# One scheduling change to a two-layer decoder step on eight cores: per-queue transfer model, moved norm, bigger weight packets

**Chip, cores, metric.** One Trainium2 chip, eight cores, each working on one prompt sequence of 2048 rows and 64 rows of decode samples; nothing is exchanged between cores. The metric is the device time of the slowest core in microseconds. Most executions agree within 0.3%.

## The reference

```python
def hybrid_layer(x, ...):
    h = rms_norm(x, norm_g)
    p = h @ w_in                                   # 1024 -> 3456 columns
    a_val, a_gate, a_z, b_h, b_b, b_c, b_z, c_u, c_v, c_z = split(p)
    # group A: GLU, causal depthwise conv of width 31, LayerNorm over 384 channels
    y_a = silu(layer_norm(causal_dwconv(a_val * sigmoid(a_gate)) + bias)) * silu(a_z)
    # group B: gated conv of width 3
    y_b = b_b * causal_dwconv3(b_c * b_h) * silu(b_z)
    # group C: LayerNorm of c_v, 128x128 causal position mixing per chunk
    y_c = c_u * chunk_mix(layer_norm(c_v)) * silu(c_z)
    return x + concat(y_a, y_b, y_c) @ w_out, ...   # plus new conv states
# two layers, then a final rms_norm; prompt and samples
```

## The kernel before

Each layer goes through the rows in five blocks of up to 512 rows. A block takes x, norms it (H_elem), transposes it (T, on TensorE), and multiplies h by pieces of w_in (stages A, Bz, AZ, CV, B, C); the GLU output goes through HBM to build the operand of the width-31 convolution; at the end mix is multiplied by w_out (stage_O), one block late. A seam is the passage from one block to the next. In the lines of the profile xr is x, h_tm and h_fm are h before and after the transposes, nv is the normed c_v, a_t the GLU output, a_scr its copy in HBM, A the operand of the width-31 convolution, and as_ext and zst are the histories of convolutions A and B for the samples; the engines are PE (TensorE), ACT (ScalarE), DVE (VectorE), GpSimd (POOL) and SP, which issues DMA. The program is written as a list of statements with reads and writes. A greedy scheduler then orders each engine's instructions by simulated times, and only that order is built.

```python
    def order(self):
        ...
        dma_free = 0.0
        while len(out) < n:
            # per engine: of the next LOOK statements that are ready, the one that can start first
            ...
            if op.dma:
                issue = 100.0 if e != "pool" else 1000.0
                free[e] = st + issue
                dstart = max(st + 1300.0, dma_free)
                dma_free = dstart + op.nbytes / 190.0      # ONE stream for all queues
                fin = dma_free + 900.0
            else:
                free[e] = st + op.cost
                ...
```

```python
        def H_elem(l, blk):                       # the norm of a block
            for j, (t, r, c0) in enumerate(blk.tiles):
                act(h_tm[...], xr[...], AF.Square, ..., accum=ss[...])   # ACT
                rsq(rstd[...], ss[...], ...)                             # GpSimd: add, pow
                ts(h_tm[...], xr[...], rstd[...], ...)                   # DVE

        def hist_dma(l, after=()):                # conv histories of the samples
            ... as_ext <- st_aT (GpSimd queue), scaled on DVE
            dma("sp", zst[:], st_bT[l], [], ["zst"], after)
            cp(zs_ext[...], zst[...], ..., eng="pool")                   # GpSimd cast

        def params_comp(l, after=()):
            S.add("pool" if l else "dve", W4 = idh32 * wc4, cost=7000 if l else 3300)   # 128x3072
```

```python
        for oi, (l, blk) in enumerate(order_b):
            stage_A(l, blk)
            a4 = [a4_load(l, blk, c, False) for c in range(3)]
            if prev is not None: stage_LN(*prev, pcb)
            ...
            stage_Bz; stage_AZ
            if prev is not None: stage_O(*prev)
            ... # loads: x of the next block; w_out in the very first block
            stage_CV(l, blk)
            mC = mark()
            if blk.first: hist_dma(l, mC)
            if nxt is not None: H_elem(*nxt)      # norm of the next block
            for c in range(3): stage_B(l, blk, c)
            stage_C(l, blk)
            if nxt is not None:                   # the seam to the next block
                convs(..., [0]); T(*nxt, 0); T(*nxt, 1)
                convs(..., [1, 2]); T(*nxt, 2); T(*nxt, 3)
                convs_smp(...)
                stage_stats(l, blk)
```

## Time and profile before

| | before |
|---|---|
| median of the first three runs | 671.95 us (671.85 to 711.28) |
| span of the cores in the profile | 662.3 to 672.4 us, median 665.9 |
| TensorE (PE) busy, slowest core | 610.5 us of 672.4 |
| PE idle between its first transposes and its last matmul, median core | about 41 us |
| start of the first w_out stage, median core | 127.4 us |

The page and the waits are read in the prediction below, with their lines. In the page's rows each digit is a fortieth of the span in tenths; a line of PE's timeline is start, length, engine, line, operation, shapes, count, and in brackets the idle time before it with what ended it. I use the start of each w_out stage as a milepost: its matmuls are easy to find in every trace, and PE does the same work between two of them in both kernels.

### The profile page before, as it was taken

What the parts mean: (1) busy time and instruction counts of PE and PEld (TensorE: products, weight loads), DVE (VectorE), ACT (ScalarE), POOL (GpSimd) and SP (SyncE); (2) the same over time, 40 slices, a digit from 0 to 9 for tenths busy, and PEclk for the clock granted to TensorE, in tenths of its full rate; (3) what the DMA queues carried; (4) which work ended last, traced back from release to release, by engine and by line L of the source; (5) the groups of instructions that cost most, each with busy time, mean ns of one, the idle gap of its engine ahead of it and who ended that gap; (6) DMA issues with size and microseconds to landing.
All of it is one profiled execution on the core that took longest, in us unless ns stands there. A gap on an engine that the chain in (4) does not pass through costs nothing.

```text
span 672.4 us, 11366 instructions; the slowest of 8 cores (662.3 to 672.4 us)
## 1 busy us (share of the span) xinstructions
PE 610.5 (91%) x4452; PEld 329.0 (49%) x4452; DVE 395.9 (59%) x742; ACT 251.8 (37%) x432; POOL 94.8 (14%) x163
## 2 busy tenths in 40 slices
PE   1779759999999999999989998999989999999974
PEld 0334324455556555555534543455545655655631
DVE  1273423964485566586485542896269576664764
ACT  3311326402630640651454034622462373272622
POOL 1601030210031011001240400121011002100101
PEclk9998959999999999999999999999979999999977
DMA  8999785842796079089494983521642033313202
GB/s 193 135 223 165 146 120 133 184 132 46 168 195 156 1 160 225 15 234 229 129 171 119 202 146 109 114 95 38 176 117 95 17 118 102 101 44 55 96 0 94
DMA packets 64053, 83.97 MB, mean 125 GB/s; under 512 B 8128, under 2 KB 54912, under 8 KB 64000
## 3 DMA queue, kind: packets, MB, share of 16 engines
q1 hardware_dynamic: 41600, 59.56, 31.2%
q0 software_dynamic: 18176, 19.24, 21.4%
q10 hardware_dynamic: 4224, 4.46, 2.6%
q8 instruction: 35, 0.57, 0.3%
q14 instruction: 18, 0.15, 0.1%
HBM read 80.59 MB, written 27.62 MB: 161 GB/s over the span
## 4 chain that ended last, share of the span: by engine, by line
PE 79%; DMA 8%; ACT 5%; DVE 4%; POOL 2%; issue 2%; SPq 0%; POOLq 0%; ACTq 0%; DVEq 0%; another core or an unknown queue 0%
PE pb L442 70%; PE pb L443 6%; DMA w_in_sb<-w_in 5%; PE pb L560 2%; DMA xr<-x_scr 2%; DMA xr<-x_in 2%; ACT tmp L402 1%; ACT L402 1%; DVE tmp L422 1%; ACT h_tm L402 1%; POOL w_in_sb L432 1%; DVE h_fm L415 1%; ACT cbh L402 1%; ACT vb L402 1%; DVE mix L410 0%
## 5 line engine op out<-in xcount | busy, mean ns | idle before, releaser
L442 PE MATMUL pb<-h_fm,w_in_sb 128*128 128x384 bf16 (+2 forms) x2000 | 374.5, 347 | 18.3 <-ACT tmp L402 4.6
L442 PEld LDWEIGHTS pb<-h_fm,w_in_sb 128*128 128x128 bf16 x2000 | 194.7, 99 | 185.6 <-issue 15.9
L402 ACT ACTIVATE tmp<-pb 128x384 f32<-128x384 f32 (+2 forms) x110 | 57.3, 522 | 264.1 <-PE pb L442 254.7
L442 PE MATMUL pb<-w_out_sb,mix 128*128 128x512 bf16 (+1 forms) x544 | 122.1, 385 | 4.0 <-DVE mix L410 4.0
L442 PEld LDWEIGHTS pb<-w_out_sb,mix 128*128 128x128 bf16 (+1 forms) x544 | 54.1, 100 | 69.8 <-DVE mix L410 4.4
L410 DVE TENSOR_TENSOR xr<-pb,xr 128x512 f32<-128x512 f32 (+1 forms) x68 | 46.5, 688 | 43.2 <-PE pb L442 43.0
L538 POOL TENSOR_SCALAR rstd<-ss 128x1 f32<-128x1 f32 (+1 forms) x47 | 12.6, 269 | 317.9 <-ACT h_tm L402 187.4
L410 DVE TENSOR_TENSOR mix<-tmp 128x384 bf16<-128x384 f32 (+2 forms) x50 | 30.0, 601 | 30.8 <-ACT tmp L402 30.6
L443 PE MATMUL pb<-A,W 128*32 128x384 bf16 (+2 forms) x1152 | 47.9, 314 | 0.1
L402 ACT ACTIVATE h_tm<-xr 128x1024 bf16<-128x1024 f32 (+1 forms) x34 | 35.6, 1049 | 11.0 <-DMA xr<-x_in 6.3
L422 DVE SCALAR_TENSOR_TENSOR tmp<-z_ext,pc,tmp 128x384 f32<-128x384 bf16 (+1 forms) x60 | 38.9, 658 | 1.2
L402 ACT ACTIVATE tmp<-xr 128x1024 bf16<-128x1024 f32 (+1 forms) x17 | 18.0, 1057 | 55.4 <-DVE xr L410 55.4
L422 DVE SCALAR_TENSOR_TENSOR tmp<-pb,pc,mean_b 128x384 f32<-128x384 f32 (+2 forms) x30 | 18.6, 652 | 33.9 <-ACT mean_b L402 33.9
L415 DVE TENSOR_SCALAR h_fm<-pb,pc 128x384 bf16<-128x384 bf16 (+2 forms) x40 | 17.2, 437 | 34.6 <-PE pb L560 32.7
L410 DVE TENSOR_TENSOR tmp<-pb,tmp 128x384 f32<-128x384 f32 (+2 forms) x50 | 29.6, 593 | 10.3 <-PE pb L442 9.6
L443 PEld LDWEIGHTS pb<-A,W 128*32 128x32 bf16 x1152 | 25.6, 96 | 20.0 <-issue 4.0
L422 DVE SCALAR_TENSOR_TENSOR a_t<-tmp,pb 128x384 bf16<-128x384 f32 (+1 forms) x30 | 16.4, 559 | 27.8 <-ACT tmp L402 27.5
L757 DVE RECIPROCAL vb<-vb 128x384 f32<-128x384 f32 (+2 forms) x10 | 27.9, 2793 | 7.7 <-ACT vb L402 7.6
L415 DVE TENSOR_SCALAR h_tm<-xr,rstd 128x1024 bf16<-128x1024 f32 (+1 forms) x34 | 25.1, 748 | 11.8 <-POOL rstd L539 7.8
L442 PE MATMUL pb<-w_in_sb,h_fm 128*128 128x256 bf16 (+1 forms) x272 | 31.6, 273 | 0.0
L402 ACT ACTIVATE h_fm<-pb,pc 128x384 bf16<-128x384 bf16 (+2 forms) x40 | 24.2, 614 | 17.3 <-PE pb L560 14.7
L402 ACT ACT_TABLE_LOAD x22 | 28.2, 1283 | 5.0 <-DMA xr<-x_in 4.7
(73 smaller groups left out, 457.4 us busy)
## 6 DMA issues: line engine op xcount, KB each, us to landing
A<-a_scr SPq DMA_DIRECT2D x96, 103.0 KB, 5.3
w_in_sb<-w_in POOLq DMA_DIRECT2D x17, 512.0 KB, 21.6
xr<-x_in SPq DMA_DIRECT2D x16, 512.0 KB, 10.0
x_scr<-xr SPq DMA_DIRECT2D x16, 512.0 KB, 5.3
xr<-x_scr SPq DMA_DIRECT2D x16, 512.0 KB, 7.9
y_o<-xr SPq DMA_DIRECT2D x16, 512.0 KB, 2.7
w_out_sb<-w_out POOLq DMA_DIRECT2D x4, 1024.0 KB, 18.7
w_in_scr<-w_in POOLq DMA_DIRECT2D x7, 512.0 KB, 13.2
```

The lines of the kernel that those rows point to most:

```text
L402: S.add("act", lambda e: e.activation(out=out, in_=in_, func=func, **kw), reads=reads, writes=writes, cost=170 + 0.833 * free_size(out) + ...
L410: S.add(eng, lambda e: e.tensor_tensor(out=out, in0=a, in1=b, op=op), reads=reads, writes=writes, cost=velem(eng, out, 1))
L415: S.add(eng, lambda e: e.tensor_scalar(out, a, s1, None, op0), reads=reads, writes=writes, cost=velem(eng, out, fast))
L422: S.add(eng, lambda e: e.scalar_tensor_tensor(out=out, in0=a, scalar=s, in1=b, op0=op0, op1=op1), reads=reads, writes=writes, cost=velem(e ...
L432: S.add(q, lambda e: e.dma_start(out=out, in_=in_), reads=reads, writes=writes, dma=True, nbytes=n * (2 if in_.dtype == BF16 else 4), afte ...
L442: return lambda e: e.matmul(out, lhsT, rhs, start=start, stop=stop)
L443: return lambda e: e.matmul(out, lhsT, rhs, start=start, stop=stop, tile_position=tp)
L538: S.add("pool", lambda e: e.tensor_scalar(out, in_, EPS, None, ALU.add), reads=rk, writes=wk, cost=300)
L560: pe([(lambda e, k=k, j=j, r=r, c0=c0: e.transpose(V[:, k % 2, c0:c0 + r], h_tm[0:r, j, k * 128:(k + 1) * 128], ident_bf[0:r, 0:r])) for k ...
L757: S.add("dve", lambda e: e.reciprocal(vb[:, 0:n], vb[:, 0:n]), reads=["vb"], writes=["vb"], cost=90 + 6.4 * n)
```

## The change

Its intent: let the scheduler believe that each queue's transfers run by themselves, move block 1's norm behind the second of three B steps, move histories and w_out of layer 0 later, start the first block with two of its four tiles, load w_in in packets twice as long, hide later seams (third convolution behind the transposes, statistics in the next stage A), and put the first tap of convolution B on ACT. Cut to its core:

```diff
+GW = [2, 4]          # groups per w_in piece, per layer (was 4, 4): 2048 B packets in layer 0
+GO = [8, 8]
+    RATE = {"sp": 180.0, "pool": 250.0, "act": 150.0}
-        dma_free = 0.0
+        dma_free = {}
-                dstart = max(st + 1300.0, dma_free)
-                dma_free = dstart + op.nbytes / 190.0
-                fin = dma_free + 900.0
+                dma_free[e] = max(st + 1300.0, dma_free.get(e, 0.0)) + op.nbytes / self.RATE[e]
+                fin = dma_free[e] + 900.0
...
-            dma("sp", zst[:], st_bT[l], [], ["zst"], after)
+            dma("sp", zst[:], st_bT[l], [], ["zst"], after if l else ())
...
-                ts(o, win(0), colA(l, c, 3), None, ALU.mult, ...)          # tap 0 on DVE
+                act(o, win(0), AF.Copy, ..., scale=colA(l, c, 3))          # on ACT
...
         for t in blocks[0].ids:
-            load_x(0, t)
+            load_x(0, t, (), "act" if t % 2 else "sp")
-        H_elem(0, blocks[0])  ... all four tiles, then the projections
+        H_elem(0, blocks[0], (), (0, 1))   ... two halves, each with half-width projections
...
-            stage_A(l, blk)
+            stage_A(l, blk, (lambda: stage_stats(*prev)) if prev is not None else None, ...)
-            if blk.first:
+            if blk.first and l:
                 hist_dma(l, mC)
-            if nxt is not None:
+            late = l == 0 and blk.first
+            if late:
+                pass
+            elif nxt is not None:
                 H_elem(*nxt)
             for c in range(3):
                 stage_B(l, blk, c)
+                if late and c == 1:
+                    H_elem(*nxt, mark())
+            if blk.first and l == 0:
+                hist_dma(l, mD)            # w_out of layer 0 likewise, behind stage_C
             stage_C(l, blk)
...
-                convs(l, blk, a4, pcb, [1, 2])
+                convs(l, blk, a4, pcb, [1])
                 T(*nxt, 2)
                 T(*nxt, 3)
+                convs(l, blk, a4, pcb, [2])
                 convs_smp(l, blk, a4, pcb, [0, 1, 2])
-                stage_stats(l, blk)
```

## The prediction

> **What bounds the kernel now.** I read the page first, then the spans of the cores, the waits of TensorE (PE), PE's timeline over the first 135 us and around the later seams, and the table of stretches.
>
> ```profile
> span 672.4 us, 11366 instructions; the slowest of 8 cores (662.3 to 672.4 us)
> PE 610.5 (91%) x4452; PEld 329.0 (49%) x4452; DVE 395.9 (59%) x742; ACT 251.8 (37%) x432; POOL 94.8 (14%) x163
> PE   1779759999999999999989998999989999999974
> PEclk9998959999999999999999999999979999999977
> DMA  8999785842796079089494983521642033313202
> ```
>
> PE is the bound, in every slice from the seventh on. The change removes no matmul of weight, so the only thing to win is PE's idle time, 672.4 - 610.5 = 62 us, and the time at the lower clock (digits 5 and 7 in the PEclk row). The first six slices, 0 to 101 us, hold most of both, and there the DMA row is full. The waits of PE say who ends the gaps:
>
> ```profile
> PE pb L560 <- DVE h_tm L415: 9.8, 1, 9.8
> PE pb L873 <- DVE ident_bf L426: 8.6, 1, 8.6
> PE pb L873 <- DVE h_tm L415: 7.5, 3, 5.6
> PE pb L442 <- ACT tmp L402: 4.6, 3, 3.3
> PE pb L442 <- DVE h_fm L415: 4.2, 4, 1.1
> PE pb L442 <- DVE mix L410: 4.0, 1, 4.0
> PE pb L442 <- DMA w_in_sb<-w_in: 4.0, 2, 3.8
> ```
>
> PE's timeline puts them in time (start, length, instructions, idle before):
>
> ```profile
> 22.78 9.22 PE L442 MATMUL pb<-h_fm,w_in_sb 128*128 128x512 bf16 x32 [2.58 <-ACT h_fm L402]
> 50.27 7.03 PE L442 MATMUL pb<-h_fm,w_in_sb 128*128 128x512 bf16 x24 [3.75 <-DMA w_in_sb<-w_in]
> 90.20 4.87 PE L560 MATMUL pb<-ident_bf,h_tm 128*128 128x128 bf16 x32 [9.82 <-DVE h_tm L415]
> 492.42 7.88 PE L442 MATMUL pb<-h_fm,w_in_sb 128*128 128x384 bf16 x30 [3.30 <-ACT tmp L402]
> 649.45 13.36 PE L442 MATMUL pb<-w_out_sb,mix 128*128 128x512 bf16 x48 [4.03 <-DVE mix L410]
> ```
>
> So there are five places: the first projection cannot start before 22.78; it runs dry of w_in at 46.5; the seam from block 0 to block 1 of layer 0 costs 9.82; a dozen seams of about 1 us each; and the tail. In the table of stretches (PE, PEld, DVE, ACT and POOL busy, granted clock, DMA share, GB/s) the seam has a second cost:
>
> ```profile
> 80.00:85.00 5.00, 0.38 (x2) 0.00 (x0) 1.68 (x4) 4.58 (x9) 2.53 (x5) 1.00 0.01 4
> 90.00:95.00 5.00, 4.80 (x32) 2.73 (x32) 1.56 (x4) 2.33 (x4) 0.00 (x0) 0.50 1.14 168
> 95.00:100.00 5.00, 3.97 (x15) 1.78 (x15) 0.90 (x2) 0.21 (x1) 0.00 (x0) 0.62 1.18 167
> ```
>
> PE waits while ACT squares block 1 (4.58 of 5 us) and DMA is idle (0.01): x landed long before, and the squares merely stand behind the last Silu of block 0 in ACT's order. Afterwards the clock is 0.50 and 0.62.
>
> **What the Trainium skill says.** (1) "TensorE: Matmul & The Clock Gate", Part 1: PE falls to half clock after about 3.4 us of idleness and needs about 3.4 us of work to return. The trace agrees: after gaps of 9.82, 3.75, 3.30 and 4.03 us the clock reads 0.50 to 0.68, after the gaps of 0.8 to 1.8 us it stays 1.00. (2) "DMA: Bandwidth & Descriptors", Issuing engines are not separate DMA queues: transfers from several engines share the same 16 DMA engines. The trace agrees: from 20 to 75 us the DMA share is 1.03 to 1.18 whoever issued, so moving x loads to ACT's queue reorders bytes and makes no bandwidth. (3) The same page, Why small descriptors are slow: a fixed cost per packet. The trace has it: cast packets of w_in take a median of 98 ns at 1024 B written and 134 ns at 1536 B, which is about 26 ns fixed plus 36 ns per 512 B written (per 1 KB of f32 read). (4) "ScalarE: Activation LUTs", What ACT_TABLE_LOAD costs: 1283 ns. The trace: 22 of them, 1283 ns mean.
>
> **The change part by part.**
>
> *Startup and w_in.* Now x0 lands at 4.65 but x1 only at 12.75 and x2 at 14.83, and the projection waits for all four tiles. After, x1 goes out at once on ACT's queue, and two tiles are normed, transposed and projected before the other two. From x1's landing (estimate 7 to 9) the chain is table load 1.28, two squares of 1.25, two roots, two scalings of 0.75, a transpose and half-width evictions: about 8.5 us, so the first half projection starts near 16 to 17. That is 6 us earlier, but the second half of its weights is piece 1, which may only be loaded once x2 is there; it landed about 25 us before, and I expect 21 to 22. So PE starts early, then waits; the 32-matmul stretch ends near 30 instead of 32.0. Then w_in: halving its packets (g of 4 becomes 2) makes one of 2 KB written cost about 26 + 144 = 170 ns instead of two of 98. A 512 KB piece is 512 x 98 / 16 = 3.1 us now and 256 x 170 / 16 = 2.7 us after; eleven pieces and the big one drop from 38.8 to 33.8 us. As a check, between 15.1 and 76.8 us all traffic (w_in 38.8, block 1's x 4.5, A loads 10.5, as_ext 4.4, rest of x and parameters 3.5) adds up to 61.7 us: that stretch is one saturated DMA. The as_ext load (4.4) is also moved behind it. Piece 6, which PE lacked at 46.5 until 50.13, then lands at 46 to 49, with the A loads of the first channel newly ahead of it. PE would ask for it near 44.5: a stall of about 3 us remains. Later pieces are no longer short. The 1.21 wait for nv goes because stage B now stands before it. Sum here: 4.5 us (2 to 8).
>
> *The seam to block 1.* H_elem of block 1 now comes after the second of three stage-B steps, so ACT's 4 x 1.24 us, POOL's 4 x 0.8 and DVE's 4 x 0.75 lie beside the third B step (3.5), the mixing (0.6), a convolution (1.9) and two CU/CZ stages (7.2), 13 us of PE. Gone: 9.82 idle, the 1.04 for h_fm, and the slow clock. The last is: from 90.20 to 100.57 PE did 32 transposes and 16 matmuls, which at full clock are 32 x 63 ns + 16 x 194 ns = 5.1 us; it took 10.4, less the 1.04 gap, so 4.2 us. Sum 15.1; I take off 1.5, since as_ext now lands about when DVE wants it, just ahead of the h_fm evictions: 13.5 (9 to 15).
>
> *Other seams.* The third convolution moves behind the last transposes and covers their evictions (1.04, 1.13 and 1.04 us at 168, 405 and 474). The statistics move into the next block's stage A: 0.80 twice and 0.28 four times. That is 5.9; I count 5. The 3.30 at 492 is ACT waiting for a late x1 load inside its order with tanh behind it. The new order has the squares after tanh and Silu, so that goes too, with its slow clock (30 matmuls at 263 ns for 176, 2.6 us), but only core 3 has it, and it is why core 3 is 6 us above the median core.
>
> *First tap of conv B on ACT.* 30 DVE operations of about 0.43 us become ACT operations of about 0.5 us. Neither engine bounds; in the tail DVE is the chain, and three taps less are about 1 us of its 4.03. But one tap there waits in ACT behind the Silu of the LayerNorm. I count 0.7.
>
> *Costs added.* Half-width matmuls add about 32 weight loads, beside the matmuls; new ACT waits in front of tanh 1 us.
>
> **Sum.** The median core is at about 666: 666 - 4.5 - 13.5 - 5 - 0.7 + 1 = 643. The slowest core was 6 above the median; without core 3's special gap I expect 2, so 645, 4% faster.
>
> **Rivals.** *The weights bind anyway.* If w_in arrives no sooner (packets twice as long at the same bytes per second; A loads earlier in the stream), PE starts early and waits longer at pieces 1 and 6, and the startup part is zero, with a slow clock behind a stall over 3.4 us. For it: the share above 1 all the way. Against it: the fixed 26 ns and the removed as_ext. Time: 650. *A wait takes the place of the seam's.* as_ext is issued about 67 us, behind w_in in the same queue, and took 18 us to land before. DVE would then block in front of h_fm, and PE stall 5 us, clock included. For it: that landing time. Against it: its own work is 4.4 us and the queue is nearly empty by then. Time: 651. *ACT becomes the new seam.* The taps and the moved statistics put ACT work in front of tanh and Silu at ten seams; 1 us more at each takes back the small seams. ACT at 40% speaks against. Time: 653. *All goes well*, piece 6 included: 634.
>
> **Range and chances.** Centre 645. The seam alone, the surest part, is 2%; startup and small seams rarely fail together. 8 in 10: 635 to 657. Faster than 2% means below 658.5: 0.93; within 2%: 0.06; slower: 0.01.
>
> **What would show it.** Right: first 256-column matmuls near 16 to 17 us; PE waiting for w_in once or twice by 3 us or less; no gap over 2 us around 75 to 85 us and PEclk 1.00 there; no wait of PE for h_fm or cbh after 110 us; PE busy down to about 600, mostly from the clock; packets of 2048 B in w_in's queue near 170 ns. Wrong: a w_in wait of over 4 us, a gap ended by h_fm with as_ext behind it, waits for ACT tmp above 6 us in sum, or a clock of 0.5 in the first 60 us that was not there before.

## The result

The changed kernel: 648.54 us median of 12 runs (645.23 to 757.17; two slow), against 672.92 us for 15 runs of the kernel before. Executions in which one die ran at a lower clock are left out of the means. The ratio of the fast runs is 0.9642, 95% interval 0.9624 to 0.966. A ratio is always the mean time of one kernel's fast runs over that of the kernel before in the same rounds, so not quite the ratio of the medians; where I turn ratios into microseconds below, I multiply by 673.

The page of the changed kernel, the same rows as those of the kernel before in the prediction:

```profile
span 645.6 us, 11435 instructions; the slowest of 8 cores (640.7 to 645.6 us)
PE 603.4 (93%) x4484; PEld 330.6 (51%) x4484; DVE 379.2 (59%) x710; ACT 269.1 (42%) x472; POOL 92.9 (14%) x163
PE   1799989999899999999989999999999999999973
PEclk9999979999999999999999999999999999999977
DMA  8999888625956395199597862531633062224102
```

The low digits of the PE row up to 100 us (before: 7, 7, 7 and 5 in slices 2, 3, 5 and 6) are gone but for slice 2, which holds the start, and an 8 in slice 6, PE's busy time fell by 7 us (I put it down to the clock, by the first digits of PEclk), and the DMA row still shows 8 and 9 up to about 110 us. PE's waits (total, times, longest) on the same core, 6, without the start's 12.3 and 1.7:

```profile
PE pb L444 <- DMA w_in_sb<-w_in: 4.7, 2, 2.9
PE pb L444 <- DVE mix L412: 4.0, 1, 4.0
PE pb L445 <- DMA A<-a_scr: 3.8, 1, 3.8
PE pb L444 <- ACT tmp L404: 3.5, 2, 1.8
PE pb L444 <- DVE a_t L424: 2.3, 1, 2.3
```

The 9.8 us for the norm of block 1 is gone, and so are the waits for h_fm on DVE. Two are new: 3.8 us for a convolution operand, and two of 1.8 us for a tanh on ACT (the kernel before had three ended by ACT tmp, 4.6 us in sum). PE's timeline puts them in time:

```profile
17.12 3.50 PE L444 MATMUL pb<-h_fm,w_in_sb 128*128 128x256 bf16 x16 [2.90 <-DMA w_in_sb<-w_in]
22.92 1.92 PE L444 MATMUL pb<-h_fm,w_in_sb 128*128 128x256 bf16 x16 [1.85 <-DMA w_in_sb<-w_in]
83.61 3.60 PE L445 MATMUL pb<-A,W 128*32 128x512 bf16 x32 [3.75 <-DMA A<-a_scr]
167.58 7.97 PE L444 MATMUL pb<-h_fm,w_in_sb 128*128 128x384 bf16 x48 [1.77 <-ACT tmp L404]
336.42 1.89 PE L444 MATMUL pb<-h_fm,w_in_sb 128*128 128x512 bf16 x8 [2.27 <-DVE a_t L424]
```

The first projection comes at 17.12 instead of 22.78, but PE then waits twice for weights. The tail's 4.0 (the wait for mix) is what it was. The gap at 80 to 83.6 us is nearly core 6's own: two other cores show 0.3 and 1.1 us there, five none, and the traces of a3, b2, b3 and f1 below, with nearly the same loads, show none on any core, while b1 has one of 3.4 us on core 1: it comes in some executions. It brings back the slow clock, as the table of stretches shows (PE, PEld, DVE, ACT and POOL busy, granted clock, DMA share, GB/s):

```profile
80.00:85.00 5.00, 1.40 (x16) 0.59 (x20) 0.79 (x2) 0.81 (x2) 0.00 (x0) 0.69 1.20 216
85.00:90.00 5.00, 5.00 (x36) 1.83 (x29) 0.00 (x0) 1.37 (x2) 0.00 (x0) 0.63 1.18 177
```

At the same place the kernel before had a DMA share of 0.01, here it is 1.20: the seam is no longer held by an order of instructions, but where it is held, by the transfers.

The mileposts, medians of the eight cores' traces, in us:

| | before | after | won so far |
|---|---|---|---|
| first projection | 23.4 | 17.2 | 6.2 |
| end of block 0's projections | 78.8 | 77.0, with a convolution of 1.85 already done | 3.7 |
| first w_out stage | 127.4 | 108.3 | 19.1 |
| second | 190.9 | 172.1 | 18.8 |
| fourth | 301.0 | 281.7 | 19.3 |
| fifth | 364.4 | 346.2 | 18.2 |
| sixth | 433.2 | 410.9 | 22.3 |
| tenth | 643.6 | 620.3 | 23.3 |
| span | 665.9 | 642.1 | 23.8 |

So four fifths of the gain are there by the first w_out stage, and all later seams together bring about 4 us, nearly all of it between the fifth and sixth stage, where the seam from block 0 to block 1 of layer 1 lies (near 405 us before). What brought those 4 us is shown under b4 below.

### The profile page after: what moved, and what is told of

The parts are those of the page before. It is cut to its first block, busy times and chain, and to the rows that moved or that the text cites. A ratio compares the mean times of both kernels' runs of the same rounds, so it can differ in the third digit from the quotient of the medians.

```text
span 645.3 us, 11435 instructions; the slowest of 8 cores (640.7 to 645.6 us)
## 1 busy us (share of the span) xinstructions
PE 604.7 (94%) x4484; PEld 331.6 (51%) x4484; DVE 381.4 (59%) x710; ACT 269.2 (42%) x472; POOL 95.0 (15%) x163
## 4 chain that ended last, share of the span: by engine, by line
PE 86%; DMA 6%; ACT 3%; DVE 2%; issue 1%; SPq 0%; POOLq 0%; POOL 0%; ACTq 0%; DVEq 0%
PE pb L444 76%; PE pb L445 7%; DMA xr<-x_in 4%; PE pb L568 3%; DMA w_in_sb<-w_in 1%; ACT tmp L404 1%; ACT L404 1%; DMA A<-as_scr 1%; DVE tmp L424 1%; DVE vb L776 0%; ACT vb L404 0%; DVE tmp L412 0%; SPq L434 0%; DVE mix L412 0%; ACT mean_b L404 0%
## 5 line engine op out<-in xcount | busy, mean ns | idle before, releaser
L444 PE MATMUL pb<-h_fm,w_in_sb 128*128 128x384 bf16 (+3 forms) x2032 | 371.6, 342 | 13.1 <-DMA w_in_sb<-w_in 5.6
L444 PEld LDWEIGHTS pb<-h_fm,w_in_sb 128*128 128x128 bf16 x2032 | 197.0, 99 | 174.3 <-issue 7.5
L543 POOL TENSOR_SCALAR rstd<-ss 128x1 f32<-128x1 f32 (+1 forms) x47 | 12.3, 261 | 333.2 <-ACT h_tm L404 221.2
L445 PE MATMUL pb<-A,W 128*32 128x384 bf16 (+2 forms) x1152 | 49.3, 314 | 1.1 <-DMA A<-as_scr 1.1
L417 DVE TENSOR_SCALAR h_fm<-pb,pc 128x384 bf16<-128x384 bf16 (+3 forms) x44 | 17.8, 417 | 34.1 <-PE pb L568 24.2
L404 ACT ACTIVATE h_fm<-pb,pc 128x384 bf16<-128x384 bf16 (+3 forms) x44 | 24.9, 582 | 17.7 <-PE pb L895 12.5
L404 ACT ACT_TABLE_LOAD x22 | 28.2, 1283 | 7.7 <-DMA xr<-x_in 7.3
L544 POOL TENSOR_TENSOR rstd<-rstd,mhalf 128x1 f32<-128x1 f32 (+1 forms) x47 | 30.7, 654 | 3.8
```

Source lines behind the costliest of these rows:

```text
L404: S.add("act", lambda e: e.activation(out=out, in_=in_, func=func, **kw), reads=reads, writes=writes, cost=170 + 0.833 * free_size(out) + ...
L417: S.add(eng, lambda e: e.tensor_scalar(out, a, s1, None, op0), reads=reads, writes=writes, cost=velem(eng, out, fast))
L444: return lambda e: e.matmul(out, lhsT, rhs, start=start, stop=stop)
L445: return lambda e: e.matmul(out, lhsT, rhs, start=start, stop=stop, tile_position=tp)
L543: S.add("pool", lambda e: e.tensor_scalar(out, in_, EPS, None, ALU.add), reads=rk, writes=wk, cost=300)
L544: S.add("pool", lambda e: e.tensor_tensor(out=out, in0=out, in1=mhalf[0:r, 0:nt], op=ALU.pow), reads=wk + ["mhalf"], writes=wk, cost=650)
```

## The experiments

Twelve kernels were run, each three or five rounds against the kernel before on the same chip. All gave right results.

| run | based on | ratio, 95% interval | us against the changed kernel (0.9642) |
|---|---|---|---|
| a1_squares_early | after | 0.9849 [0.9825, 0.9872] | +13.9 |
| a2_model_only | before | 0.9807 [0.9775, 0.9839] | +11.1 |
| a2c_model_late | before | 0.9897 [0.9873, 0.9921] | +17.2 |
| d1_history_late | before | 0.9794 [0.9772, 0.9816] | +10.2 |
| a3_small_packets | after | 0.9687 [0.9666, 0.9709] | +3.0 |
| b1_one_phase | after | 0.9624 [0.9584, 0.9664] | -1.2 |
| b2_old_seams | after | 0.9672 [0.9649, 0.9696] | +2.0 |
| b3_tap_dve | after | 0.9639 [0.9609, 0.9668] | -0.2 |
| b4_old_model | after | 0.9931 [0.9905, 0.9957] | +19.5 |
| c1_x1_on_act | after | 0.9723 [0.9702, 0.9744] | +5.5 |
| e2_w4_dve | c1 | 0.9659 [0.9637, 0.9681] | +1.1 |
| f1_w4_and_stats | after | 0.9577 [0.9541, 0.9613] | -4.4 |

### What moves the squares: the model or the statement?

The prediction credits the moved H_elem. A build without a run already spoke against that: the kernel before with the late H_elem alone gives ACT, SP and GpSimd the very same order of instructions as before. The reason is in the order of ACT's work. Kernel before, core 3, ACT's timeline:

```profile
80.42 0.60 ACT L402 ACTIVATE tmp<-pb 128x512 f32<-128x512 f32 x1 [1.13 <-PE pb L442]
80.91 1.05 ACT L402 ACTIVATE h_tm<-xr 128x1024 bf16<-128x1024 f32 x1
```

The first square of block 1 (h_tm<-xr) comes after the last Silu of block 0 (tmp<-pb). With one common stream for all queues, the scheduler believes that x of block 1 lands behind all the megabytes issued before it, and finds no square ready in time, wherever the statement stands.

**a2_model_only**: the kernel before with the new model only.

```diff
+    RATE = {"sp": 180.0, "pool": 250.0, "act": 150.0}
...
-                dma_free = dstart + op.nbytes / 190.0
+                dma_free[e] = max(st + 1300.0, dma_free.get(e, 0.0)) + op.nbytes / self.RATE[e]
...
```

> The kernel before with one thing changed: the scheduler models each queue's transfers by themselves, instead of one common stream. No statement is moved. Theory A (the transfer model alone moves the squares of block 1 ahead of block 0's last Silus, because it stops believing that x lands late): the 9.8 us wait of PE near 80 us is gone, and the time falls by 8 to 15 us against the kernel before, perhaps less if the squares now stand too early. Rival B (the moved statement does it, the model is incidental): within 3 us of the kernel before and the wait near 80 us still there.

Measured: 0.9807, 13.0 us below the kernel before. The wait near 80 us is gone on all cores and the first w_out stage comes at 117.0 instead of 127.4. Theory A holds. The edit changes the assumed rates too, and no run parts the two; builds without a run do, as far as the order goes. With three queues at the old 190 each, the first square of block 1 stands at place 17 of ACT's order, with the new rates at 18, in the kernel before at 27, and with one stream at 250 at 26. So the separate queues move it, and not the rates. It is not free: the squares now stand a little too early (on core 3 ACT stands 13.1 us for x of block 1). PE's waits on core 3:

```profile
PE pb L442 <- ACT tmp L402: 8.3, 3, 3.1
PE pb L442 <- DVE nv L418: 4.8, 1, 4.8
```

Seven cores lose 1.0 to 7.1 us in front of nv at 65 to 73 us. The second seam also got worse: from the first to the second w_out stage it takes 67.4 us, where the kernel before took 63.5.

**b4_old_model**: the reverse, the changed kernel with the old model.

```diff
-                dma_free[e] = max(st + 1300.0, dma_free.get(e, 0.0)) + op.nbytes / self.RATE[e]
+                dma_free = max(st + 1300.0, dma_free) + op.nbytes / 190.0
...
```

> The changed kernel with the scheduler's old transfer model, one common stream for all queues; no statement is moved. The run with the model alone gained 12 us on the kernel before. Theory A (the model is one of the parts that make the gain, by what it lets the order be around the first seam): 8 to 15 us slower than the changed kernel, with a gap of PE of 4 us or more between 60 and 95 us. Rival B (with the statements moved, the order is forced, and the model adds little): within 3 us of the changed kernel.

Measured: 0.9931, that is 19.5 us of the changed kernel's 24 lost, more than theory A asked for. The gap at the seam is 7.9 us on all eight cores, and the first w_out stage comes at 126.8. ACT's timeline of this run on core 6 has nearly the old order again, all statements of the change in place (only the last Silu stands behind the first square):

```profile
78.36 0.60 ACT L404 ACTIVATE tmp<-pb 128x512 f32<-128x512 f32 x1 [4.97 <-PE pb L444]
78.86 1.05 ACT L404 ACTIVATE h_tm<-xr 128x1024 bf16<-128x1024 f32 x1
79.89 0.59 ACT L404 ACTIVATE tmp<-pb 128x512 f32<-128x512 f32 x1
```

whereas in the changed kernel, core 6, the squares begin 11 us before the last Silus of the block, the first of which is the second line:

```profile
62.41 1.05 ACT L404 ACTIVATE h_tm<-xr 128x1024 bf16<-128x1024 f32 x1
73.23 0.60 ACT L404 ACTIVATE tmp<-pb 128x512 f32<-128x512 f32 x1 [2.95 <-PE pb L444]
```

The model also explains the gain between the fifth and sixth w_out stage (medians of the eight cores): 68.8 us in the kernel before and 68.7 here, but 64.5 with the model alone (a2), 64.7 in the changed kernel and 64.5 in it with the old seams (b2 below). So those 4 us, at the seam from block 0 to block 1 of layer 1, are the model's and not those of the moved convolution and statistics, and they are part of why this run lost more than expected.

So the line that matters most costs no time on the chip at all: it is a belief about transfers.

### What the late statement is for

**a1_squares_early**: the changed kernel without it.

```diff
-            late = l == 0 and blk.first
+            late = False
```

> The changed kernel with one thing undone: the norm of block 1 (squares on ACT) is again stated ahead of the three B steps of block 0, with no tie to the second of them; the new transfer model of the scheduler stays. Theory A (the late tie is needed: without it the scheduler puts the squares in front of ACT work of block 0 while block 1's x is still landing near 60 to 66 us, and ACT stands there): 5 to 12 us slower than the changed kernel, with a PE wait of several us between 50 and 75 us. Rival B (the order of the squares against the last Silus is all that counts, and the tie is only caution): within 1.5 us of the changed kernel, block-1 projection near 84 us.

Measured: 0.9849, 13.9 us slower than the changed kernel, a little beyond theory A's range and at the place it names. ACT's timeline on core 4:

```profile
63.86 1.06 ACT L404 ACTIVATE h_tm<-xr 128x1024 bf16<-128x1024 f32 x1 [17.75 <-DMA xr<-x_in]
```

ACT stood 17.75 us for x of block 1, with tanh, Silu and evictions of block 0 behind that square in its strict order. PE waited 4.6 us for a tmp of ACT and then 6.4 for nv, and its first w_out stage came at 124.5 instead of 108.3. The per-queue model is too hopeful about x (it forgets that the queues share the engines), and the late statement is the guard against that. Why its absence costs more here than in a2, where the model alone still gains, was not traced.

**a2c_model_late**: the kernel before, the model, and the late statement.

```diff
+            late = l == 0 and blk.first
...
+                if late and c == 1:
+                    H_elem(*nxt, mark())
```

> The kernel before with two things changed: the per-queue transfer model and the late statement of block 1's norm (after the second B step). Theory A (these two are the whole of the seam's gain): 12 to 17 us below the kernel before, PE gap near 80 us under 2 us and the granted clock 1.0 there. Rival B (the seam also needs the moved convolution, statistics and history load): 5 to 10 us below the kernel before, with a gap of 3 us or more left at the seam. If it equals the run with the model alone, the late statement is idle.

Measured: 0.9897, 6.9 us below the kernel before, with a gap of 5.9 to 9.8 us at the seam. That is what rival B said (5 to 10 us, a gap of 3 us or more), and it is 6 us slower than the model alone. The chain of waits of core 0 (start, length, what) says why:

```profile
73.69 11.53 DMA zst<-st_bT
85.27 0.27 POOL zs_ext L426
85.63 0.23 POOL rstd L538
...
92.62 2.46 PE pb L561 x16
```

The 48 KB load of the B history took 11.5 us, the cast that waits for it stands ahead of the norm's roots in GpSimd's order, and the whole norm stands behind that cast. I had feared such a wait for as_ext on DVE; it comes from its small neighbour on GpSimd, and only as long as the history is not moved as well. So of the three parts that rival B names it is the history load; the next run tests it.

**d1_history_late**: the same with the history moved as in the change.

```diff
-            dma("sp", zst[:], st_bT[l], [], ["zst"], after)
+            dma("sp", zst[:], st_bT[l], [], ["zst"], after if l else ())
...
-            if blk.first:
+            if blk.first and l:
                 hist_dma(l, mC)
...
+            if blk.first and l == 0:
+                hist_dma(l, mD)
             stage_C(l, blk)
```

> The run with the transfer model and the late norm on the kernel before, with one more part of the change: the history of layer 0 (the as_ext and zst loads) is moved as in the change, zst to the start and as_ext behind the third B step. In the run without it PE stood 5.9 to 9.8 us at the seam because GpSimd's cast of zst, ahead of the norm's roots in its order, waited for a 48 KB load that took 11.5 us. Theory A (the late norm and the history move belong together; alone the first is undone by that load): the gap goes, the first w_out stage near 113 to 117 us instead of 123.0, and the time is 5 to 9 us below the run without it, so 12 to 16 below the kernel before. Rival B (the seam is bound by something else, for example GpSimd's issue of the w_out loads ahead of the roots): a gap of over 4 us remains and the time is within 2 us of the run without it.

Measured: 0.9794, 6.9 us below a2c_model_late; the gap at the seam is 0.3 us at most on every core, and the first w_out stage comes at 113.4. Theory A holds. Late norm and moved history belong together: with both, the model's gain goes from 13.0 to 13.9 us (the intervals overlap, so no gain over the model alone is shown); with the late norm alone it falls to 6.9. The moved history without the late norm was not run.

### The weights and the start

**a3_small_packets**: the changed kernel with four groups per piece again.

```diff
-GW = [2, 4]
+GW = [4, 4]
```

> The changed kernel with the weights of both w_in layers in pieces of four groups again (packets of 1024 B written instead of 2048 B for layer 0); instruction orders are otherwise the same. Theory A (the bigger packets bring w_in earlier, as the prediction counted: 5 us over the eleven pieces): PE's waits for w_in in the first 55 us grow by 3 to 5 us in sum, piece 6 among them, and the time by 3 to 6 us with the slower clock. Rival B (bytes bind, not packets, or the weights are hidden): within 1 us of the changed kernel.

Measured: 0.9687, 3.0 us slower, at the low end of theory A. The first w_out stage comes at 112.9, 4.6 us later on the median core. PE's waits of core 0 in this run and then of core 0 in the changed kernel:

```profile
PE pb L444 <- DMA w_in_sb<-w_in: 10.0, 4, 5.1
```

```profile
PE pb L444 <- DMA w_in_sb<-w_in: 4.1, 3, 2.4
```

The 5.1 us stall on a middle piece at 56 us is back. In the packet records of the GpSimd queue the median packet takes 98 ns at 1024 B and 173 ns at 2048 B (134 and 247 ns at 1536 and 3072 B): the prediction's 170 was right. A 512 KB piece thus takes 512 x 98 / 16 = 3.1 us of all engines before and 256 x 173 / 16 = 2.8 after.

**b1_one_phase**: the changed kernel with the start in one phase, all four tiles first.

```diff
-        H_elem(0, blocks[0], (), (0, 1))
-        ... two halves of transposes, evictions and 256-column projections
+        H_elem(0, blocks[0])
+        ... all transposes and evictions at once
+        pre = []
```

> The changed kernel with the startup in one phase again: all four tiles of block 0 are normed and transposed before the first projection, at full width; x still comes over two queues and all else stays. Theory A (the half-width start is what brings the first projection forward, 23 to 17 us): the first projection near 21 to 23 us, the end of block 0 some 2 to 4 us later, time 2 to 4 us above the changed kernel. Rival B (the weights bind: in the changed kernel PE starts early only to wait 4.7 us for w_in): within 1 us, because the full-width start uses fewer, longer matmuls and meets weights that have landed.

Measured: 0.9624 [0.9584, 0.9664], no difference from the changed kernel that these rounds can show. Rival B holds within that. The first projection is back at 23.8 us (median), 6.6 later, and no wait for w_in is left in its slowest core's list, where the changed kernel has 4.7 us (three other cores have one of 2.3 to 2.9 us near 65 us). Block 0 ends at 77.7 instead of 77.0. Starting early mostly turned a wait for h into a wait for weights.

### The later seams and the tap

**b2_old_seams**: statistics and the second and third convolutions as before.

```diff
-            stage_A(l, blk, (lambda: stage_stats(*prev)) if prev is not None else None, ...)
+            stage_A(l, blk, None, ...)
-                convs(l, blk, a4, pcb, [1])          # [2] behind T(*nxt, 3)
+                convs(l, blk, a4, pcb, [1, 2])
+                stage_stats(l, blk)
```

> The changed kernel with the later seams undone: the statistics stand at the end of a block again, and the second and third convolutions stand together before the last transposes. Theory A (the prediction: the moves remove 5 us of small waits for h_fm, cbh and sq, and cost nothing): 4 to 6 us slower, with waits of about 1 us for h_fm at each seam of a convolution block. Rival B (they only move the wait: the changed kernel shows new waits of 1.8 us for a tanh behind the evictions of the convolution, twice): 1 to 3 us slower, and the two 1.8 us waits near 163 and 466 us gone.

Measured: 0.9672, 2.0 us slower, though the intervals just overlap (by the tenth w_out stage the median core is 3.3 us later). Rival B's size. The waits for h_fm, cbh and sq are back, as the 1.0, 0.8 and 0.3 us of before, but not at the seam near 405 us, which the model had already cleared. But the moves also cost: between the fourth and fifth w_out stage this kernel takes 62.1 us and the changed one 64.5, since the 2.3 us wait for a_t near 334 us isn't there with the old order. Rival B's sign was only half right: the 1.8 us waits near 163 and 466 us are not gone but are 1.5 to 3.0 us here (the ones named ACT tmp).

**b3_tap_dve**: the first tap on DVE again.

```diff
-                act(o, win(0), AF.Copy, [key, "pc"], [k2], scale=colA(l, c, 3))
+                ts(o, win(0), colA(l, c, 3), None, ALU.mult, None, [key, "pc"], [k2])
```

> The changed kernel with the first tap of convolution B on DVE again, PE's order the same. Theory A (neither engine binds; only the tail has DVE in its chain): 0 to 1 us slower, the last wait of PE 4.0 us becomes about 4.5 to 5. Rival B (the tap costs more on ACT than it saves, since ACT's queue stands in front of tanh): 1 us faster or more, and the waits for ACT tmp shrink.

Measured: 0.9639, no difference. The tail's wait is 4.03 us in both, not the 4.5 to 5 of theory A. Only a gap of 0.23 us ahead of the last eight projections comes back. DVE's 13 us less and ACT's 18 us more are beside PE's work.

### The new gap of core 6, and what else to win

Two edits aimed at the changed kernel's own waits. The 3.75 us gap of core 6 follows a store of the convolution's input that took 28 us to land. Chain of waits, changed kernel, core 6:

```profile
46.79 28.21 DMA a_scr<-a_t
...
76.36 7.21 DMA A<-a_scr
```

**c1_x1_on_act**: x of block 1 on ACT's queue, w_out behind the transposes.

```diff
-                    load_x(nxt[0], t, mA)
+                    load_x(nxt[0], t, mA, "act" if oi == 0 else "sp")
...
-            if blk.first and l == 0:              # behind stage_C
-                for hf in range(2):
-                    load_wout(0, hf, mark())
+                if late:                          # behind T(*nxt, 3)
+                    for hf in range(2):
+                        load_wout(0, hf, mark())
```

> The changed kernel with block 1's x loads on ACT's queue instead of SP's, and the w_out loads of layer 0 issued behind the last transposes of the seam. Theory A (the one new gap of the changed kernel, 3.75 us on core 6 near 80 us and 0.3 to 1.1 us on two others, is the store of the convolution's input standing behind x loads in SP's ring): that gap goes on all cores, the slowest core gains 2 to 5 us, the time 1 to 3 us. Rival B (all queues share the same engines, so the queue doesn't matter, only the bytes ahead): the store still lands over 20 us after its issue and the time is within 1 us.

Measured: 0.9723, 5.5 us slower: a miss. The gap near 80 us is gone on all cores, but that says little, as it is absent in the traces of a3, b2, b3 and f1 too. The store still took 25.1 us on core 6, as rival B said (22.2 to 28.7 on the eight cores of the changed kernel); PE merely came to that convolution 4 us later. And w_out, issued at 84.6 instead of 75.2 us, now runs beside what the next seam needs: x of block 2 was issued at 102.2 and took 11.6 us, where the changed kernel issues it at 98.5 and has it in 5.5. Chain of waits, core 6:

```profile
102.17 11.59 DMA xr<-x_in
```

ACT's first square waits for it and the rest of ACT and DVE behind it; PE stands 2.5 to 4.5 us in the first w_out stage on all cores, with a slow clock after it on six of them. The two edits were not run apart. Whether another order of these loads would take the 3.75 us off core 6 for nothing stays open.

**e2_w4_dve**: on top of c1, two edits. The 2.3 us wait for a_t near 334 us has a cause that no wait names. Changed kernel, core 6, DVE's timeline and then GpSimd's:

```profile
329.49 6.19 DVE L412 TENSOR_TENSOR mix<-tmp,szt 128x384 bf16<-128x384 f32 x2
```

```profile
329.48 5.78 POOL L497 TENSOR_TENSOR W<-cst,wc 128x3072 bf16<-128x3072 f32 x1 [8.49 <-PE pb L444]
```

Two DVE products of 0.55 us each took 6.19 us together, begun with GpSimd's product and ended 0.4 us after it. The Trainium skill explains it, "SBUF — State Buffer", SBUF: two separate sides: DVE and GpSimd share a port pair under an exclusive lock held for the whole instruction, and a DVE operation with two SBUF inputs needs it. The trace agrees: the DVE operation has two SBUF inputs and stood for the 5.78 us.

```diff
+            if l == 0:
+                w4_comp(after)                    # the 128x3072 product, on DVE
...
             stage_AZ(l, blk)
+            if blk.first and l:
+                w4_comp(mB)                       # layer 1: on DVE too, where DVE is idle
...
-                if c == 0 and mid is not None:
+                if c == (1 if prev is not None and prev[1].smp else 0) and mid is not None:
                     mid()                         # the statistics, one channel later
```

> The kernel of the run with x on ACT's queue, with two more edits: the 128x3072 product of layer 1 runs on DVE behind stage AZ instead of on GpSimd, and the statistics of the block with samples stand behind the second instead of the first channel of the next stage A. Theory A (the 2.3 us wait of PE near 334 us comes from DVE standing still while GpSimd runs that 5.8 us product; the two 1.8 us waits come from a root with two table loads ahead of a tanh): the 2.3 us wait goes, the 1.8 us ones shrink, 2 to 5 us faster than the run with x on ACT's queue. Rival B (DVE's own 3.4 us product blocks just as well, and the root only moves to another wait): within 1.5 us of it, with waits of the same size elsewhere.

Measured: 0.9659, 4.3 us faster than c1. All three waits are gone. **f1_w4_and_stats** is the same two edits on the changed kernel, without c1's.

> The changed kernel with only the two edits that worked on top of the run with x on ACT's queue: layer 1's 128x3072 product on DVE behind stage AZ, and the statistics of the block with samples one channel later; x and w_out stay as in the changed kernel. On top of the other kernel these two gave a ratio of 0.9659/0.9723 = 0.993. Theory A (they remove waits on PE that stand on the path whatever the start does: 2.3, 1.8 and 1.8 us): 4 to 6 us below the changed kernel's ratio of 0.9642, so a ratio near 0.957 and about 644 us, with no wait for DVE a_t near 334 us or ACT tmp near 163 and 467 us. Rival B (the gain of that run came from the other start, by luck of the order): within 1.5 us of the changed kernel.

Measured: 643.23 us median, ratio 0.9577, 4.4 us below the changed kernel with intervals that don't meet: the best version. PE's waits on its slowest core, without the start's first:

```profile
PE pb L444 <- DMA w_in_sb<-w_in: 5.7, 2, 3.8
PE pb L444 <- DVE mix L412: 4.7, 2, 4.0
PE pb L444 <- DVE z L412: 1.1, 1, 1.1
```

No ACT tmp and no a_t is left; what remains there after the start is the tail and under 3 us of small waits (core 7 has one of 2.9 us for mix near 470 us). The two edits were not run one by one; by the mileposts (median cores, against the changed kernel) 1.9 us come between the first and second w_out stage, where only the statistics moved, and 2.8 between the fourth and fifth, where only the product did.

## Why the prediction was right, and where it was not

- **Total.** 645 predicted, 648.5 measured, within the range. The prediction counted in spans of the trace: its median core was to be at 643 and is at 642.1, its slowest at 645 and is at 645.6. The timed runs lie a little above that: the profiled run itself was timed at 647.7, 2.1 us above the span of its slowest core. The agreement of the sum is in part luck, since the causes behind two of its terms were others than it names, as follows.
- **Startup and w_in, 4.5 predicted, 3.7 measured** (end of block 0, less the convolution). The first projection near 16 to 17 us was right (17.2), and so was the packet time. But the half-width start, which filled most of that paragraph, brought nothing that shows (b1); the packets make the term (a3: 3.0 us). Of the rival that the weights bind anyway, one half came true (PE starts early, then waits for the first pieces), the other did not (with the longer packets w_in does arrive sooner). The predicted stall of 3 us at piece 6 did not come; instead the first pieces were later than expected, 17 and 22.9 us. (One reading is slightly off: the DMA share from 20 to 75 us reaches 1.19, not 1.18.)
- **The seam to block 1, 13.5 predicted.** From the end of block 0's projections to the first w_out stage 15.4 us were won (19.1 - 3.7). The size was right and so was what lies beside what, and the prediction had read rightly that the squares merely stood behind the last Silu in ACT's order. The step that failed is what moves them: it said that H_elem of block 1 "now comes after the second of three stage-B steps" and so lies beside PE's work. The order of the changed kernel has that, yet the statement alone moves nothing; the scheduler's new transfer model, which the prediction's sum does not mention, does (13.0 us alone; 19.5 lost without it, 4 of the latter at the same seam of layer 1), the late statement keeps the squares from standing too early (13.9), and the history has to move with it (6.9). These numbers don't add up, because each part is a condition for the others.
- **The rival wait for as_ext** did not come in the changed kernel: as_ext landed 8.2 us after its issue. The rival was right about the danger: a2c shows it, with zst and GpSimd in place of as_ext and DVE.
- **Other seams, 5 predicted, 2.0 measured for the moves** (b2, intervals just overlapping). From the first w_out stage to the end the median core won 4.7 us, so the size came out, but 4 of these lie at the seam near 405 us and are the model's (a2, b2, b4). The removed waits were as listed; what the step left out is that the moves make a new wait by a lock between DVE and GpSimd (2.3 us near 334, where the kernel before had 1.8) and two of 1.8 for a tanh, 3.5 us in sum where I had set 1. That is the ACT rival, on a small scale. Core 3's gap at 492 us went, as predicted.
- **The tap, 0.7 predicted, about 0 measured** (b3). The tail's 4.03 us does not depend on it.
- **Core 6's gap** at 80 us was not foreseen: a store whose landing takes 28 us. It costs that core 3.75 us and a slow clock (0.69 and 0.63), and it breaks one of the prediction's signs of being right, no gap over 2 us around 75 to 85 us. The slowest core hardly owes its time to it: core 1, without the gap, ends at 645.3 us against its 645.6.

## What to carry to other kernels

Where a scheduler decides the order, its model of transfers is worth as much as any statement: look at the built order before crediting a moved line, and run the model change alone. A part that looks useless or harmful by itself may be the condition of another, so try pairs (the late norm cost 6 us as long as the history was not moved, and taking it away from the whole change cost 14). And when a short instruction takes ten times its usual length, look at what the other engines did in that very interval; the waits will not name it.

## What the Trainium skill lacked or had wrong

- "TensorE: Matmul & The Clock Gate", Part 1, names about 3.4 us of idleness for the fall to half clock. Here shorter gaps were enough at times: in c1_x1_on_act, after a gap of 2.60 us on core 6 the granted clock was 0.55 over the next 2 us, while on core 2 it stayed 1.00 after one of 3.3 us. So a gap of 2.6 us is already a risk, and one of 3.3 us no certainty.
- "ScalarE: Activation LUTs", What ACT_TABLE_LOAD costs, adds a drain of about 1380 ns to the 1283 ns of the load itself. The load's time agrees; of the drain these traces show nothing: in the changed kernel a load from 163.76 us on takes 1.28 us and the root after it starts at 165.06, so a root between other functions costs 2.6 us of loads, not over 5.
- "DMA: Bandwidth & Descriptors", Why small descriptors are slow: it gives no time per packet for casting loads from GpSimd's queue. Measured medians are 98, 134, 173 and 247 ns at 1024, 1536, 2048 and 3072 B written, so about 23 ns fixed and 75 ns per KB.
- No page that I read says how long a small transfer takes to land when other transfers are in front of it: a 48 KB load took 11.5 us and a 128 KB store 28 us here, and moving the neighbouring loads to another queue left the store at 25 us, in line with "DMA: Bandwidth & Descriptors", Issuing engines are not separate DMA queues.
